# Six weight products in a row on TensorE: five of every six go ahead of all other matmuls in its order

## The chip, the cores and the metric

The kernel runs on one core of one Trainium2 chip. The metric is the device time of one execution in microseconds; the median of several runs counts. Nothing is shared with another core, and there are no collectives.

## The reference

One inference step of a four-layer decoder for two groups of tokens that share the weights: a prompt of 256 tokens and 8 samples of 4 tokens, together 288 columns. Each layer is

```python
x = x + 0.5 * _swiglu(_rmsnorm(x, g0), w_in0, w_out0)
x = x + mixer(_rmsnorm(x, gm))
x = x + 0.5 * _swiglu(_rmsnorm(x, g1), w_in1, w_out1)
```

and the mixer is, by layer, windowed attention with sinks ("swa", layers 0 and 3), the gated delta rule ("gdn", layer 1) and the HGRN2 recurrence ("hgrn", layer 2). The width is 1024, the hidden width of the FFN 2816, everything in 32-bit floats. Every mixer has an input projection, work on heads, states and caches, and an output projection.

## The kernel before

All projections go through one class, `Stream`. A projection is cut into jobs. A job is a column of up to four 128x128 weight tiles ("k tiles") that are multiplied with 288 columns of activations and added up in one PSUM bank. To keep the precision, a weight tile is split into a high part `hi` (ScalarE, line 71) and a rest `lo` (VectorE, line 72), and the activations into `xh` and `xl` likewise; a k tile then takes three products, hi·xh (line 97), hi·xl (line 98) and lo·xh (line 99). So a job of four k tiles is twelve products, and the whole kernel has 16,152 of them. They are called **weight products** here. Up to two jobs ahead are split, three banks (`acc`) take sums, and a finished sum is read by an evacuation function (`evac`) on VectorE, ScalarE or GpSimd.

All other matmuls are called **mixer matmuls**: scores, transposes, decays, states, the inverses of the delta rule, norms. Many of them do not use the whole array. Lines 530, 1190 and 1192 have 64 rows, lines 545, 572, 875, 1167 and 1181 have 64 columns, lines 1098, 1415, 1474 and 1478 have 32. They are called **narrow** here, and those with 128 rows and 128 columns **full**. In the profile a form such as 128*64 is rows * columns of the weights.

The order of each engine's instructions is fixed when the program is built. A list scheduler walks a modelled execution: whenever an engine is free it takes, of the instructions whose inputs are there by the model, the one with the lowest priority number. The number is the place in the program, less an offset where the code sits in `tc.high_priority(offset)`. On the chip each engine then executes its list strictly in that order, and waits where an input is not there yet. `tc.issue_after(ins)` puts instructions behind `ins` in the list of its engine.

The weight products of before stand at their place in the program, without an offset. The mixer work of gdn and hgrn is written after projections that do not depend on it, and raised with offsets: `PRIO = 5000` for the cores of the delta rule and for the heads of hgrn, 6000 to 6500 (`SP`, `QP`, `QG`) for others. So a mixer matmul goes into PE's list as soon as its input is there, between any two weight products. Evacuations, splits and loads have priorities of their own.

Dependencies that matter below: in swa the second half of the output projection (eight jobs) needs all heads; in gdn the last input group (`z1`, 16 jobs) and the first half of the output projection (16 jobs) are left to run beside the cores of heads 4 to 7, and the second half needs those; in hgrn the first half of the output projection (eight jobs) needs heads 0 to 3 and the second half heads 4 to 7. The matmuls of a norm are put behind the products `mms[11]`, `mms[13]` and `mms[25]` of the first eight jobs, where `mms` has the third product of each k tile.

Of the kernel before, what the change touches and what calls it, by code (L numbers as in the profile page):

```python
# [24 lines left out]
class Stream:  # L25
# [3 lines left out]
    def __init__(self, tc, raw, split, psum):  # L29
        self.tc, self.nc, self.raw, self.split_pool, self.psum = tc, tc.nc, raw, split, psum  # L30
        self.chunks, self.jobs = [], []
        self.loaded, self.tiles, self.left = 0, {}, {}
        self.nsplit, self.parts = 0, {}
        self.njob = 0
        self.accs = {}
        self.pooled = set()
        self.held, self.mms, self.tags = [], [], {}
        self.loads = {}
        self.first = 0

    def chunk(self, loads):
        self.chunks.append(loads)
        return len(self.chunks) - 1
# [41 lines left out]
    def run(self, count, hold=False):  # L85
        self.mms = []
        for j in range(self.njob, self.njob + count):
            self.split_to(j + 1 + AHEAD)
            chunk, view, nk, xs, acc, start, stop, evac, m = self.jobs[j]
            hi, lo = self.parts.pop(j)  # L90
            if start:
                self.accs[acc] = self.psum.tile([128, 512], F32, tag=self.tags.pop(acc, "acc"), name="acc")
            ps = self.accs[acc][:m, :T]
            mm = self.nc.tensor.matmul
            last = len(xs) - 1
            for i, (xh, xl) in enumerate(xs):
                mm(ps, hi[:, i, :m], xh(), start=start and i == 0, stop=False)  # L97
                mm(ps, hi[:, i, :m], xl(), start=False, stop=False)  # L98
                self.mms.append(mm(ps, lo[:, i, :m], xh(), start=False, stop=stop and i == last).ins)  # L99
            self.njob += 1  # L100
            if stop and hold:
                self.held.append((evac, self.accs.pop(acc)))
            elif stop:
                evac(self.accs.pop(acc))


PRIO = 5000
# [4 lines left out]
def trunk(ctx: ExitStack, tc: tile.TileContext, I, consts, O):  # L112
# [1547 lines left out]
    for k, run in zip(seq, runs):  # L1660
        if k[0] == "f":
            run()
        else:
            with tc.tile_pool(name="mix", bufs=1, reuse_waits="tile") as M[0]:
                run()
# [92 lines left out]
```

## Time and profile before

| | us |
|---|---|
| median of 3 runs | 2638.93 |
| lowest and highest of them | 2638.28, 2644.87 |
| the profiled execution | 2632.71 |
| its span, first to last instruction | 2630.9 |

PE has 20,268 matmuls, and of these 5384 stand at each of the lines 97, 98 and 99. Times in the rows below are microseconds from the start of the span. PE is the matmuls, PEld the loads of their weights. A matmul's duration in the trace runs over that of the next one, so what one costs is read from the distance between two starts. [...]

### The profile page before, as it was taken

The numbers are of one execution on the slowest core, as the hardware profiler recorded it, in microseconds if no ns is written. First come the engines' busy times: TensorE is split into PE (matmuls) and PEld (weight loads), VectorE is DVE, ScalarE is ACT, GpSimd is POOL, SyncE is SP. The second block draws the span as 40 slices with busy tenths as digits, with TensorE's granted clock in tenths as the row PEclk, the third lists the DMA queues.
The fourth block names the chain that finished last, engine by engine and source line by source line (L and its number), as shares of the span: only waits on it lengthen the run. The fifth ranks groups of instructions, "written<-read, shape, count | busy, mean of one in ns | idle before, by whom it ended". The sixth has DMA issues, their size and how long they took to land.

```text
span 2630.9 us, 52770 instructions
## 1 busy us (share of the span) xinstructions
PE 2549.8 (97%) x20268; PEld 2411.8 (92%) x20268; DVE 1763.5 (67%) x3772; ACT 1414.1 (54%) x3129; POOL 246.4 (9%) x404
## 2 busy tenths in 40 slices
PE   8999999999998899999999999888999999999998
PEld 8999799999997776789999999677999999979998
DVE  6666776576567867667666666877765766667655
ACT  5555655455455456755555545665554555465543
POOL 1000000000002135410000000443000000010000
PEclk9999999999999999999999999999999999999999
DMA  6655245555553354455555555333555565534553
GB/s 188 196 168 172 65 143 164 165 168 161 166 163 97 109 152 136 136 176 159 167 163 163 168 163 160 106 119 122 164 165 164 164 202 177 168 94 121 161 168 124
DMA packets 442609, 400.15 MB, mean 152 GB/s; under 512 B 24730, under 2 KB 440212, under 8 KB 442356
## 3 DMA queue, kind: packets, MB, share of 16 engines
q1 hardware_dynamic: 441732, 395.66, 49.9%
q8 instruction: 159, 2.61, 0.4%
q10 hardware_dynamic: 624, 1.11, 0.1%
q14 instruction: 94, 0.77, 0.1%
HBM read 374.64 MB, written 22.07 MB: 151 GB/s over the span
## 4 chain that ended last, share of the span: by engine, by line
PE 78%; issue 11%; DVE 6%; POOL 2%; ACT 2%; DMA 1%; DVEq 0%; POOLq 0%; ACTq 0%; SPq 0%
PE acc L97 23%; PE acc L99 23%; PE acc L98 23%; DVE lo L72 1%; PE s L545 1%; PE c L530 1%; PE c L1186 0%; DVE W L1400 0%; PE ma L537 0%; PE c L1190 0%; DVE F L1366 0%; PE c L1192 0%; PE c L1181 0%; PE c L1474 0%; ACT hi L71 0%
## 5 line engine op out<-in xcount | busy, mean ns | idle before, releaser
L97 PE MATMUL acc<-sl,hi 128*128 128x288 f32 x5384 | 1612.4, 300 | 13.0 <-ACT sl L1506 2.8
L98 PE MATMUL acc<-sl,hi 128*128 128x288 f32 x5384 | 1606.1, 298 | 1.8 <-DVE sl L1507 1.8
L99 PE MATMUL acc<-sl,lo 128*128 128x288 f32 x5384 | 1600.8, 298 | 2.4 <-DVE lo L72 2.4
L71 ACT ACTIVATE hi<-raw 128x512 fp32r<-128x512 f32 (+1 forms) x1378 | 854.3, 621 | 963.0 <-PE acc L98 934.4
L72 DVE TENSOR_TENSOR lo<-raw,hi 128x512 fp32r<-128x512 f32 (+1 forms) x1378 | 948.4, 689 | 571.2 <-ACT hi L71 515.1
L97 PEld LDWEIGHTS acc<-sl,hi 128*128 128x128 f32 x5384 | 1016.4, 189 | 26.2 <-issue 11.5
L99 PEld LDWEIGHTS acc<-sl,lo 128*128 128x128 f32 x5384 | 1021.2, 190 | 14.6 <-issue 10.0
L98 PEld LDWEIGHTS acc<-sl,hi 128*128 128x128 f32 x5384 | 1018.9, 189 | 12.8 <-issue 9.2
L276 POOL TENSOR_TENSOR r<-v,roots 128x3 f32<-128x3 f32 x5 | 5.8, 1164 | 1847.2 <-DVE v L296 1847.2
L366 DVE TENSOR_TENSOR sil<-acc,sil 128x288 f32<-128x288 f32 x176 | 79.7, 456 | 54.8 <-PE acc L99 51.3
L359 DVE TENSOR_TENSOR sil<-acc,rbc 128x288 f32<-128x288 f32 x176 | 79.6, 456 | 50.1 <-PE acc L99 49.8
L368 DVE TENSOR_TENSOR sl<-sil,sl 128x288 fp32r<-128x288 f32 x176 | 78.9, 452 | 0.0
L360 ACT ACTIVATE sil<-sil 128x288 f32<-128x288 f32 x176 | 77.6, 445 | 2.1 <-DVE sil L359 2.0
L367 ACT ACTIVATE sl<-sil 128x288 fp32r<-128x288 f32 x176 | 77.6, 445 | 0.0
L700 DVE SCALAR_TENSOR_TENSOR acc<-buf,cw,acc 128x312 f32<-128x312 f32 x96 | 59.0, 625 | 11.9 <-ACT acc L698 11.5
L246 ACT ACTIVATE sl<-x,gT 128x288 fp32r<-128x288 f32 x96 | 51.0, 536 | 26.2 <-DVE x L383 15.3
L249 DVE SCALAR_TENSOR_TENSOR sl<-x,gT,sl 128x288 fp32r<-128x288 f32 x96 | 50.5, 530 | 0.1
L262 ACT ACTIVATE sq<-x 128x288 f32<-128x288 f32 x91 | 38.7, 430 | 5.1 <-DVE x L383 5.1
L515 ACT ACTIVATE e<-e,m 128x128 f32<-128x128 f32 (+1 forms) x72 | 32.6, 454 | 16.1 <-DVE m L512 15.8
L1131 POOL TENSOR_TENSOR st<-st,ex 128x512 f32<-128x512 f32 x32 | 37.4, 1190 | 18.1 <-PE ma L1098 18.1
L259 DVE TENSOR_TENSOR ssq<-ssq,sq 128x288 f32<-128x288 f32 x84 | 37.8, 450 | 0.1
L512 DVE CUSTOM_DVE_ANT_0 e<-c,sl,sink 128x128 f32<-128x128 f32 (+1 forms) x72 | 27.8, 418 | 10.6 <-PE c L530 7.7
(435 smaller groups left out, 1823.3 us busy)
## 6 DMA issues: line engine op xcount, KB each, us to landing
raw<-in_ffn_w_in_dram SPq DMA_DIRECT2D x352, 512.0 KB
raw<-in_ffn_w_out_dram SPq DMA_DIRECT2D x128, 512.0 KB
raw<-in_ffn_w_out_dram SPq DMA_DIRECT2D x64, 384.0 KB
raw<-in_gdn_w_in_dram SPq DMA_DIRECT2D x48, 512.0 KB
raw<-in_hgrn_w_in_dram SPq DMA_DIRECT2D x32, 512.0 KB
out_dram<-st SPq DMA_DIRECT2D x24, 512.0 KB
raw<-in_swa_w_in_dram SPq DMA_DIRECT2D x32, 256.0 KB
raw<-in_swa_w_out_dram SPq DMA_DIRECT2D x32, 256.0 KB
```

What stands on the lines that cost most here:

```text
L71: self.nc.scalar.activation(out=h, in_=src, func=AF.Copy)
L72: (self.nc.gpsimd if j in self.pooled else self.nc.vector).tensor_tensor(out=l, in0=src, in1=h, op=ALU.subtract)
L97: mm(ps, hi[:, i, :m], xh(), start=start and i == 0, stop=False)
L98: mm(ps, hi[:, i, :m], xl(), start=False, stop=False)
L99: self.mms.append(mm(ps, lo[:, i, :m], xh(), start=False, stop=stop and i == last).ins)
L246: S.activation(out=h[m], in_=x[:, m], func=AF.Identity, scale=g)
L359: V.tensor_tensor(out=t, in0=ps[:, :T], in1=nrm[key]["rbc"], op=ALU.mult)
L360: S.activation(out=t, in_=t, func=AF.Silu)
L366: V.tensor_tensor(out=t, in0=ps[:, :T], in1=t, op=ALU.mult)
L367: S.activation(out=h, in_=t, func=AF.Copy)
L368: V.tensor_tensor(out=l, in0=t, in1=h, op=ALU.subtract)
L700: V.scalar_tensor_tensor(out=a[:, 0:312], in0=b[:, t:t + 312], scalar=cw[:, 32 * t + mt:32 * t + mt + 1], in1=a[:, 0:312], op0=ALU.mult, o ...
```

## The change

One attribute is added, and the three products of a k tile get offsets:

```diff
+        self.follow = 3 * PRIO
...
             for i, (xh, xl) in enumerate(xs):
-                mm(ps, hi[:, i, :m], xh(), start=start and i == 0, stop=False)
-                mm(ps, hi[:, i, :m], xl(), start=False, stop=False)
-                self.mms.append(mm(ps, lo[:, i, :m], xh(), start=False, stop=stop and i == last).ins)
+
+                with self.tc.high_priority(i % 2 * self.follow):
+                    mm(ps, hi[:, i, :m], xh(), start=start and i == 0, stop=False)
+                with self.tc.high_priority(self.follow):
+                    mm(ps, hi[:, i, :m], xl(), start=False, stop=False)
+                    self.mms.append(mm(ps, lo[:, i, :m], xh(), start=False, stop=stop and i == last).ins)
```

Of the k tiles 0 and 1 of a job, and again of 2 and 3, the first product keeps its place, and the five behind it get an offset of 15,000, more than any mixer work has. Once the first is in PE's list, the other five follow before anything else that is ready. The arithmetic, the number of instructions, the buffers and the DMAs stay as they are. A job of three k tiles is a group of six and one of three.

## Rows read from the trace of the kernel before

**Rows 1.** The page: busy time of each engine, and the chain by engine.
```profile
PE 2549.8 (97%) x20268; PEld 2411.8 (92%) x20268; DVE 1763.5 (67%) x3772; ACT 1414.1 (54%) x3129; POOL 246.4 (9%) x404
PE 78%; issue 11%; DVE 6%; POOL 2%; ACT 2%; DMA 1%; DVEq 0%; POOLq 0%; ACTq 0%; SPq 0%
```

**Rows 2.** Windows: length, busy (instructions) of PE, PEld, DVE, ACT, POOL; PEclk, DMA, GB/s.
```profile
400.00:450.00 50.00, 50.00 (x377) 50.00 (x376) 31.69 (x55) 25.62 (x47) 0.00 (x0) 1.00 0.55 164
...
244.00:341.00 97.00, 93.97 (x715) 76.19 (x714) 64.76 (x231) 54.09 (x165) 10.94 (x20) 0.95 0.32 85
790.00:950.00 160.00, 141.68 (x1499) 121.52 (x1498) 118.15 (x365) 78.96 (x185) 29.08 (x91) 0.95 0.41 111
950.00:1145.00 195.00, 185.99 (x1497) 139.16 (x1496) 138.06 (x332) 134.17 (x460) 94.98 (x148) 1.00 0.51 141
1645.00:1820.00 175.00, 150.43 (x1783) 120.32 (x1782) 138.06 (x345) 112.22 (x355) 70.21 (x96) 0.97 0.39 117
2299.00:2394.00 95.00, 92.18 (x719) 75.08 (x718) 64.30 (x232) 55.28 (x167) 11.80 (x18) 0.96 0.31 84
```

**Rows 3.** Timeline of PE in gdn: start, us, line, tiles, rows*columns, count.
```profile
1064.13 0.30 PE L97 MATMUL acc<-sl,hi 128*128 128x288 f32 x1
...
1064.39 0.38 PE L1116 MATMUL ma<-rh,t 128*128 128x128 f32 x2
1064.53 0.38 PE L99 MATMUL acc<-sl,lo 128*128 128x288 f32 x1
1064.75 0.29 PE L97 MATMUL acc<-sl,hi 128*128 128x288 f32 x1
1064.97 0.66 PE L1181 MATMUL c<-co,sl 128*64 128x128 f32 x8
1065.56 0.40 PE L98 MATMUL acc<-sl,hi 128*128 128x288 f32 x1
1065.80 0.38 PE L1116 MATMUL ma<-rh,t 128*128 128x128 f32 x2
1066.11 0.43 PE L1181 MATMUL c<-co,sl 128*64 128x128 f32 x2
1066.48 0.40 PE L99 MATMUL acc<-sl,lo 128*128 128x288 f32 x1
```

**Rows 4.** Timeline of PEld, the weight loads, in the same stretch.
```profile
1064.13 0.19 PEld L98 LDWEIGHTS acc<-sl,hi 128*128 128x128 f32 x1
...
1065.56 0.19 PEld L98 LDWEIGHTS acc<-sl,hi 128*128 128x128 f32 x1 [0.17 <-issue]
```

**Rows 5.** Timeline of PE: first and last mixer matmuls of the five mixer windows.
```profile
246.94 0.30 PE L485 MATMUL ma<-cst,sl 128*128 128x128 f32 x1 [0.95 <-DVE sl L462]
...
2388.88 0.30 PE L574 MATMUL s<-pt,new 8*64 8x32 f32 x2
```

**Rows 6.** Waits of PE in the whole span: us in total, times, longest us.
```profile
PE c L875 <- DVE sl L880: 8.1, 2, 7.8
PE c L1415 <- DVE W L1400: 5.7, 4, 3.0
...
PE c L1186 <- ACT co L1183: 4.0, 8, 1.3
...
PE ma L1051 <- ACT v L704: 0.2, 1, 0.2
```

**Rows 7.** Timelines: last mixer matmuls of swa, gdn, hgrn (PE), last gating product (POOL).
```profile
334.75 0.42 PE L574 MATMUL s<-pt,new 8*64 8x32 f32 x2
...
1142.27 0.27 PE L1211 MATMUL s<-cst,co 128*128 128x128 f32 x1
...
1150.36 3.19 POOL L1228 TENSOR_TENSOR sl<-sl 128x512 f32<-128x512 f32 x2 [4.65 <-ACT sl L1221]
...
1819.44 0.30 PE L1500 MATMUL s<-lmask,o 128*128 128x32 f32 x2
```

**Rows 8.** Window of 5 us right behind the last matmuls of swa; columns as in Rows 2.
```profile
335.50:340.50 5.00, 5.00 (x22) 5.00 (x22) 1.30 (x3) 0.63 (x1) 0.89 (x2) 0.50 0.05 15
```

## The prediction, made before the change was run

> **What bounds the kernel now.** I read the page first. PE is busy 97% of the span, it carries 78% of the chain that ended last, and no other engine has more than 6% of that chain [rows 1]. So a change of PE's order can move the time, in both directions. Next I read the windows, to see where PE has anything to reorder. In an FFN stretch 377 products take 50 us, 0.133 us each, with PE and PEld busy all the time; nothing else is on PE there, and six in a row are what already runs [rows 2]. The norms' few matmuls are tied to `mms[11]`, `mms[13]` and `mms[25]`, each the last product of a group of six (the fourth, second and second k tile of its job), so their places stay too. What is left are the five mixer windows of together 722 us [rows 2].
>
> Then I followed PE's timeline through these windows, from the first mixer matmul to the last of [rows 5], and counted. The row of weight products is broken 322 times: 46, 40, 112, 75 and 49 times in the five windows in their order. In 209 of these breaks a narrow matmul stands. Only 53 breaks stand at a multiple of six. Of the 321 rows of products between breaks, 209 have fewer than six, on average some 2.5.
>
> **What a break costs.** The excerpt [rows 3] shows both kinds. A full matmul costs its own time and no more: from 1064.39 to 1064.75 two of line 1116 and one product take 0.36 us, which is 0.133 and twice 0.11. Its weights load while the product ahead runs, as a product's do: the load for line 98 starts at 1064.13 with the product of line 97 [rows 3, 4]. A narrow burst costs more at both edges. The product ahead of it takes 0.22 us (1064.75 to 1064.97), 0.09 more than 0.133; the product behind it takes 0.24 us (1065.56 to 1065.80), 0.11 more. Its weights aren't loaded ahead either: PEld idles 0.17 us and starts at 1065.56 together with its own product [rows 4]. Inside, eight narrow ones take 0.59 us and two take 0.37 us (1066.11 to 1066.48), so 0.037 each and 0.30 per burst. If two bursts come to stand at one place, 0.20 us is saved surely, and 0.50 at most, where the two also share the 0.30. I take 0.30, near the lower end, since most neighbours are of different lines and wait for each other's results.
>
> [...]
>
> **The change, part by part.** It adds no instruction, no DMA and no semaphore, and leaves the queues of SP, ACT, DVE and POOL their priorities. It moves products two to six of a group past whatever mixer matmuls were ready, whether these have an offset or not. A mixer matmul that stood within a group now stands up to five products later, by turns 0 to 0.67 us, on average 0.33. Three terms follow.
>
> *Merged breaks, a gain.* If each break moves to the next multiple of six and nothing else moves, the 209 places with narrow matmuls become 153. 56 places times 0.30 us are 17 us (11 to 28 with the ends above). But a delayed matmul delays the one that depends on it, and opens a new break there. That leaves between nothing and all of it; I take half, 8 us.
>
> *Shorter waits, a gain.* PE works its list strictly in order, and the list was made from a model. So PE stands still at mixer matmuls whose inputs come later than modelled: without the one stall at line 875, 55 such waits with together 39 us [rows 6], where the first rows and the last of the list stand. A matmul that is 0.33 us later in the list, behind weight products that are ready, shortens its wait by as much; capped by each row's mean wait this is 18 us. Nothing is gained where the input moves later too. Between 0 and 18 I take 12: line 1415, which weighs most, waits for DVE and POOL work that is late because DVE is busy (138 of 175 us in hgrn [rows 2]), not because PE was late; line 1186 [rows 6] hangs on a chain through PE, and keeps part of its wait. The stall of 7.8 us at line 875 hangs on the solver's long row of steps on DVE; 0.33 us don't touch it. I leave it as it is.
>
> *Work used up early, a loss.* Weight products are what PE does between two links of a mixer chain. If each row of fewer than six, or between two multiples, is filled up, a mixer stage draws products forward: 150, 117, 353, 241 and 164 in the five windows. That costs nothing while independent products are left. Behind the last core of gdn at 1142.27 some 44 products of `z1` are left and 192 of the first half of the output, 236 in all, and the gating that the second half needs ends at 1153.5 [rows 7]. Behind the last head of hgrn at 1819.44 it is 68 and 96, so 164 [rows 7]. Behind the last attention matmul of swa at 334.75 [rows 7] it is only 38, up to the second half of the output projection. In the window from 790 DVE is the busier one in its later part, and the projections that follow are there to fill; nothing is lost. Once the reserve is gone, each further link of the chain leaves PE idle for as long as the mean row filled before. With all rows filled, swa would have done (270+38)/(270+150) = 0.73 of its 46 rows, 12 rows are left, of 270/46 = 5.9 products or 0.78 us each: 10 us, and 10 in the second swa. The same working gives 9 us for the cores of gdn (427 products in 111 rows, 17 rows left) and 7 for hgrn (545 in 75, 7 rows left). That is 36 us, the upper end; zero is the lower. With half of the rows filled, which fits half of the breaks merged, the cores need 176 of 236 and hgrn 120 of 164: nothing. The two swa need 75 and 82 against 38 and lose 4 us each: 8 us.
>
> A wait for a late `lo` stops PE with mixer work queued behind it, but in the strict list of before it did so too: zero, with the waits above as its upper end.
>
> Sum: -8 -12 +8 = **-12 us**. The profiled execution took 2632.7 us, 1.8 more than its span and 6.2 less than the median; so 2620.7 against it, and **2627 us** as a median.
>
> **The rivals.** *The chains are delayed and the reserves run out* (slower). Every row is filled, no break merges, as each link finds its group of six begun. Then 36 us are lost, and of the waits, which sit on the same chains, half is saved, 9 us, where the forecast has 12: +27, 2666 us with everything; with hgrn and gdn keeping their reserve, +20 - 9 = +11, 2650 us. It decides from the point where swa draws more than some 75 products forward in each layer. For it: the short rows are where one link waits for the next. Against it: several heads run side by side, so a delayed matmul finds company.
>
> *The clock* (slower). The granted clock has half-speed stretches in the mixer windows: from the means 0.95, 0.95, 1.00, 0.97 and 0.96 they add up to twice (4.9 + 8 + 0 + 5.3 + 3.8), 44 us [rows 2]. Behind the narrow matmuls that end at 335.1 the clock is 0.50 and a product takes 5.00/22 = 0.227 us [rows 7, 8], so all of them cost up to 44 x (1 - 0.133/0.227) = 18 us. Bigger narrow bursts could bring as many again: -12 + 18 = +6, 2645 us, and more if nothing merges. [...]
>
> *PE isn't what ends these stages* (no change). DVE is busy 138 of 175 us in hgrn and 118 of 160 in the first gdn window [rows 2]. If its chains end the stages, the gains fall into idle time: 2637 us, with what merges in swa and the cores alone eaten by swa's loss. That the order hardly moves, because the model has few mixer matmuls ready together, gives 2639 as well.
>
> *Everything merges* (faster). 17 + 18 us and no loss: 2604 us.
>
> **How the numbers follow.** A measurement of this kernel tells about 0.3%, 8 us, from no change. Forecast (2613 to 2634): 0.50, of which 0.38 below 2631. Everything merges (2600 to 2613): 0.12. PE isn't the end, or the order hardly moves (2632 to 2645): 0.18. Chains delayed (2647 to 2666): 0.14. Clock (2640 to 2655): 0.06, taken as slower. So faster 0.50, within 0.3% 0.30, slower 0.20. The range that leaves out two in ten goes from 2606 to 2652.
>
> **What would show it.** Right: breaks at multiples of six only, some 230 to 280 instead of 322, places with narrow matmuls down from 209 to about 180; the 55 waits well under 39 us; the FFN windows unchanged at 377 products in 50 us; the gain in the windows of gdn's cores and hgrn, little in swa. Wrong: PE idle ahead of the second half of swa's output projection; more than 44 us at half clock; or a new long stall like the one at line 875, since the list is made anew and can set a matmul badly: one of 8 us takes away two thirds of the gain.

## The result, and the profile after

The changed kernel takes **2665.16 us** (median of 4 runs, 2664.38 to 2665.46) where the kernel before took 2640.31 beside it (2638.28 to 2644.87): ratio 1.0091, with a 95% interval from 1.0078 to 1.0104. It is slower, by 25 us. The forecast was 2627, 12 us faster, with a range up to 2652. The forecast was wrong.

The page of the changed kernel, in the order of [rows 1] (busy time and instructions of each engine; the chain by engine; what the granted clock was in 40 slices of 66.6 us each):

```profile
PE 2574.8 (97%) x20268; PEld 2432.2 (91%) x20268; DVE 1751.7 (66%) x3772; ACT 1410.2 (53%) x3129; POOL 237.8 (9%) x404
...
PEclk9999899999999977799999999999999999999999
...
PE 80%; issue 11%; DVE 5%; ACT 2%; POOL 2%; DMA 1%; POOLq 0%; DVEq 0%; ACTq 0%; SPq 0%
```

PE is busy 25.0 us longer than in [rows 1] with as many matmuls, and three slices in the middle have a clock of 0.7. The span is 2663.6 us, 32.7 more than before. The profiled execution of before took 2632.71 us, 7.6 less than the median beside it, that of after 2665.39, its median; that is why 25 us between the medians are 33 between the two traces. A stage that differs by a few us between two traces proves nothing by itself.

Where the time went is read best from the stages, from the first weight product of one to the first of the next. PE's busy time is the union of its matmuls, and half clock the time in which the granted TensorE clock was half of the full one, both added up from the trace's records. The clock records of these two traces (22 before, 32 after) hold 1 and 0.5 of the full clock and nothing between, so a PEclk between in a window is a mean.

| stage | before: us, PE idle, half clock | after: us, PE idle, half clock |
|---|---|---|
| five FFN stretches together | 1699.7, 0.1, 0 | 1699.7, 0.1, 0 |
| swa, first | 123.0, 3.0, 10.2 | 123.5, 2.5, 17.1 |
| gdn | 422.6, 27.9, 17.1 | **466.0**, 39.3, **116.1** |
| hgrn | 238.9, 29.1, 17.1 | **229.5**, 26.5, 10.2 |
| swa, second | 120.5, 2.8, 6.8 | 118.2, 2.1, 6.8 |

The whole loss is in gdn, 43.4 us, and hgrn gains 9.4. The windows of the changed kernel that answer to [rows 2] (length, then busy time and instructions of PE, PEld, DVE, ACT, POOL, then PEclk, DMA share, GB/s; 956 to 1157 and 1157 to 1190 together answer to 950 to 1145, in which the cores of gdn run):

```profile
400.00:450.00 50.00, 50.00 (x377) 50.00 (x377) 31.82 (x56) 25.73 (x48) 0.00 (x0) 1.00 0.54 161
244.00:341.00 97.00, 94.47 (x712) 77.19 (x711) 63.98 (x229) 53.50 (x163) 11.23 (x19) 0.91 0.33 86
790.00:956.00 166.00, 146.03 (x1508) 127.28 (x1508) 118.34 (x365) 79.28 (x183) 28.61 (x93) 0.90 0.42 111
956.00:1157.00 201.00, 182.84 (x1245) 134.52 (x1243) 113.80 (x282) 113.59 (x388) 74.80 (x132) 0.80 0.39 109
1157.00:1190.00 33.00, 32.40 (x258) 25.34 (x255) 24.05 (x55) 23.55 (x75) 11.94 (x12) 1.00 0.54 161
1690.00:1855.00 165.00, 143.21 (x1779) 115.51 (x1779) 138.37 (x343) 110.29 (x350) 69.51 (x94) 0.99 0.41 123
2334.00:2427.00 93.00, 90.90 (x720) 74.80 (x720) 63.54 (x231) 55.36 (x165) 9.76 (x17) 0.96 0.33 88
```

The v projection of gdn (the value heads, 384 products) lies across two of these windows. From its first product to the first product behind it, in the changed kernel and then in the kernel before:

```profile
919.50:1120.50 201.00, 180.39 (x1501) 136.88 (x1499) 106.86 (x263) 105.04 (x337) 68.47 (x140) 0.79 0.44 119
```

```profile
920.90:1083.70 162.80, 153.96 (x1463) 117.83 (x1460) 109.82 (x261) 105.56 (x351) 73.80 (x133) 0.99 0.55 151
```

The v projection is what became slow: 201 us instead of 163, at a clock of 0.79 instead of 0.99, with nearly as many matmuls (1501 and 1463). PE was busy for 180.4 us of it instead of 154.0, 26.4 more, and idle for 20.6 instead of 8.8, 11.8 more.

The order did become what the diff says. The rows of weight products are broken 191 times in the five mixer windows, where the prediction counted 322, and 184 of these breaks stand at a multiple of six; places with narrow matmuls (all forms but 128*128) fell from 209 to 153, the number that the prediction gave for merging in full.

What a slow stretch looks like is plain from PE's timeline (start, us, line, tiles, rows*columns; the products are now at lines 100, 102 and 103, other lines four further on). A product that starts at 1016.13 is the last for 27.7 us:

```profile
1016.13 0.29 PE L103 MATMUL acc<-sl,lo 128*128 128x288 f32 x1
1016.26 0.40 PE L1144 MATMUL ma<-w,km 128*128 128x256 f32 x2
1017.90 0.74 PE L1144 MATMUL ma<-w,km 128*128 128x256 f32 x4 [1.24 <-POOL km L1139]
...
1024.75 1.93 PE L1102 MATMUL ma<-st,sl 128*32 128x256 f32 x16
1026.61 1.01 PE L1185 MATMUL c<-co,sl 128*64 128x128 f32 x8
...
1033.14 1.12 PE L1185 MATMUL c<-co,sl 128*64 128x128 f32 x8
1034.19 0.80 PE L1144 MATMUL ma<-w,km 128*128 128x256 f32 x2
1036.23 0.80 PE L1144 MATMUL ma<-w,km 128*128 128x256 f32 x2 [1.24 <-POOL km L1139]
...
1043.85 0.61 PE L100 MATMUL acc<-sl,hi 128*128 128x288 f32 x1
```

Eight matmuls of line 1185 (line 1181 of before) take 1.05 us here (1033.14 to 1034.19); in [rows 3] eight of them took 0.59. The 16 of line 1102 are recorded with 1.93 us at 1024.75, and elsewhere in the same trace, at 1109.38 and full clock, with 1.07. So PE's chain matmuls run at little more than half speed in this stretch.

Why no product was there is answered by POOL and, in the last row, DVE (same columns):

```profile
1025.91 2.04 POOL L1135 TENSOR_TENSOR st<-st,ex 128x512 f32<-128x512 f32 x2 [1.98 <-PE ma L1102]
...
1028.33 2.04 POOL L1135 TENSOR_TENSOR st<-st,ex 128x512 f32<-128x512 f32 x2
1030.33 1.04 POOL L1139 TENSOR_TENSOR km<-kr,cst 128x512 fp32r<-128x512 f32 x1
1035.14 1.04 POOL L1139 TENSOR_TENSOR km<-kr,cst 128x512 fp32r<-128x512 f32 x1 [3.77 <-PE ma L1144]
1036.14 0.69 POOL L280 TENSOR_TENSOR af<-av,roots 128x2 f32<-128x2 f32 x1
1036.78 0.10 POOL L696 MEMSET buf<- 128x3 f32 x1
...
1040.55 0.41 DVE L698 TENSOR_TENSOR buf<-acc,rbc 128x256 f32<-128x256 f32 x1
```

The products of v's columns 8, 9 and 10 had ended by 1004, 1011 and 1016, and filled the three banks. The evacuation of column 8 needs the buffer that line 696 prepares, and that memset stands on POOL behind the state work of a head (lines 1135, 1139), which hangs on the sample chain on PE (the steps of a head that read and update the samples' state). It came at 1036.78. On DVE the evacuation stood behind the same state work (line 1146) and a core's steps (lines 1199 and 1204), and came at 1040.6; the next product came at 1043.85, in PE's order behind further core matmuls. The two halves of the next weights had been ready since 1011.7. There are four such stretches in v, ahead of columns 3, 7, 11 and 15 (935 to 947, 969 to 980, 1016 to 1044, 1076 to 1106); the longest in the v of before is 5.5 us.

So the heads and the evacuations stand in another order than before, on engines of which the diff says nothing. Why, the runs below found out. In all tables the gdn stage is the one of the profiled execution, and half clock is that of the gdn stage.

### The profile page after: what moved, and what is told of

Same layout as the page of the kernel before. It is cut to its first block, busy times and chain, and to the rows that moved or that the text cites. A ratio compares the mean times of both kernels' runs of the same rounds, so it can differ in the third digit from the quotient of the medians.

```text
span 2663.6 us, 52772 instructions
## 1 busy us (share of the span) xinstructions
PE 2574.8 (97%) x20268; PEld 2432.2 (91%) x20268; DVE 1751.7 (66%) x3772; ACT 1410.2 (53%) x3129; POOL 237.8 (9%) x404
## 4 chain that ended last, share of the span: by engine, by line
PE 80%; issue 11%; DVE 5%; ACT 2%; POOL 2%; DMA 1%; POOLq 0%; DVEq 0%; ACTq 0%; SPq 0%
PE acc L100 24%; PE acc L102 23%; PE acc L103 23%; DVE lo L73 1%; PE c L534 1%; DVE W L1404 1%; PE c L1190 1%; PE c L1194 1%; PE c L1185 1%; PE s L549 1%; PE c L1196 0%; PE ma L541 0%; PE ma L1144 0%; POOL st L1135 0%; DVE F L1370 0%
## 5 line engine op out<-in xcount | busy, mean ns | idle before, releaser
L704 DVE SCALAR_TENSOR_TENSOR acc<-buf,cw,acc 128x312 f32<-128x312 f32 x96 | 52.9, 576 | 12.5 <-ACT acc L702 12.3
L386 DVE TENSOR_TENSOR res<-acc,rh 128x288 f32<-128x288 f32 x64 | 29.0, 453 | 40.7 <-PE acc L103 40.7
```

The costliest lines, as they stand in the source:

```text
L704: V.scalar_tensor_tensor(out=a[:, 0:312], in0=b[:, t:t + 312], scalar=cw[:, 32 * t + mt:32 * t + mt + 1], in1=a[:, 0:312], op0=ALU.mult, o ...
```

## The experiments

### Two runs with offsets in one layer only

The theories at the start were: A, links of the sample chain are delayed by groups of six; B, the clock falls where products are used up early; C, any list that is made anew can be bad. The first two runs set the offset to zero in gdn alone, and everywhere but in gdn.

```diff
         def run():
+            st.follow = 0
...
                 st.run(32 - 2 * KS)
+            st.follow = 3 * PRIO
```

> The change everywhere but in the gdn layer (there all offsets are 0, as before). Common to all theories, from the two traces: the gdn stage alone grew by 43.5 us (777.7 to 1200.3 before, 778.8 to 1244.8 after), hgrn shrank by 9.5, the second swa by 2.2, the first grew by 0.3. If the stages are independent of each other this kernel takes some 11 us less than the one before, about 2629 us. If the loss were spread over the span, or came from code of all stages, it would lie above 2640 us.

Measured: 2656.57 us (2648.55 to 2664.45), ratio 1.0061 [1.0041, 1.0082]; gdn 465.6 us with 112.6 at half clock, hgrn 231.5. **Miss.** In gdn no product had a real offset, and gdn was nearly as slow as with it (the traced execution took 2664.45 us, 8 over the median). Theory A can't be the cause.

The second run had the two values exchanged:

> The change in the gdn layer alone. If the stages are independent: the kernel before plus 43.5 us, about 2684 us, slower than the changed kernel itself. If the gains and losses are not tied to stages: between 2640 and 2665 us.

Measured: 2688.22 us (2678.36 to 2694.09), ratio 1.0177 [1.0152, 1.0202]; gdn 457.0 with 85.3, hgrn 236.8. The number was near the expected one, but not for its reason alone: the FFN stretches between the mixers took 427.3, 426.4 and 426.8 us instead of 424.1, 423.3 and 423.5, with an offset of 0. In PE's list third products there change places with first ones of the next k tile. So `high_priority(0)` around products isn't the same as nothing around them. In gdn PE's list is that of the changed kernel, and still the stage took 457.0 us in this trace and 466.0 in that one: so much can lie between two executions of one order.

### Raising the chain, and a smaller offset

```diff
-        SP = 6000
+        SP = 20000
...
-        CP, VP, RP = 0, 3000, 0
+        CP, VP, RP = 0, 20000, 20000
```

> The changed kernel, but in gdn the units of the sample chain (value transposes, sample unit, state update) get an offset of 20,000, more than the five products' 15,000, so that their matmuls may stand within a group of six. Theory A (links of this chain are delayed by groups of six; eight heads, one after the other, 22 us each before and 28 after): the period goes back to 22 to 24 us and most of the 43.5 us come back, 2622 to 2640 us. Theory B (the half clock in stretches of narrow matmuls is what costs, and the groups bring these stretches about by using up the products early): the cores' matmuls still wait for groups and the three banks still fill early, so at least 60 of the 97 us more at half clock stay, and the time stays above 2650 us. Theory C (the list is made from a model that misjudges, and any new list is as likely bad): no telling, anything from 2630 to 2690 us.

Measured: 2651.42 us (2643.05 to 2654.98), ratio 1.0037 [1.0027, 1.0047]; gdn 453.7 with 88.7. That is far from what theory A expected and just within what theory B did (above 2650 us, at least 60 of the 97 us more at half clock): putting the chain ahead of the products gives back 12 of 43 us.

```diff
-        self.follow = 3 * PRIO
+        self.follow = 1000
```

> The changed kernel with an offset of 1000 in place of 15,000: the five pass only work that has no offset (swa, and in gdn the state update and the convolutions), while raised work (cores of gdn 5000, sample unit 6000, heads of hgrn 5000) may stand within a group as before. Theory A: of the links of the sample chain only those of the state update are still delayed, so the gdn stage loses some 10 to 20 us in place of 43, and the gain in hgrn, whose heads are raised, is gone: 2645 to 2660 us. Theory B: short rows of products between raised matmuls come back, the clock stays up: 2635 to 2645 us. Theory C: anything.

Measured: 2666.58 us (2663.01 to 2667.52), ratio 1.0097 [1.0082, 1.0112]; gdn 457.3 with 75.1, hgrn 237.4. Neither expectation was met. With an offset under that of the heads, hgrn's gain is gone, as theory A has it, but gdn stays slow.

### What an offset of zero changes

The place numbers by which the list is made show what I had overlooked: behind a `high_priority` block the count goes on from where the block began. What stands in a block takes no number, so a number is not simply the place in the program less an offset. In the kernel before the products were nearly all that moved the count on in the v projection, since the evacuations (`conv`, a convolution), heads and sample chains stand in blocks already; in the changed kernel next to nothing does.

```
numbers of the first to the last instruction   before          after
evacuation of v column 0                       7680 to 7692    1824 to 1836
evacuation of v column 1                       7704 to 7716    1824 to 1836
evacuation of v column 2                       7730 to 7742    1826 to 1838
evacuation of v column 3                       7754 to 7770    1826 to 1842
evacuation of v column 5                       7804 to 7816    1828 to 1840
evacuation of v column 7                       7854 to 7870    1830 to 1846
sample chain of head 1, without its offset     7763 to 7795    1835 to 1867
sample chain of head 3, without its offset     7863 to 7895    1839 to 1871
```

Two columns, one head, are 50 numbers apart before and 2 after, while an evacuation is 12 to 16 numbers long and a sample chain 32. So the first steps of a later head get lower numbers than the last steps of an earlier one, on every engine, and heads overtake each other. In PE's list it is seen in how many of gdn's 1560 products stand ahead of the first matmul of each v head:

| kernel | heads 0 to 7 | gdn, half clock |
|---|---|---|
| before | 705, 756, 796, 828, 872, 926, 976, 1022 | 422.6, 17.1 |
| after | 732, 768, **864, 864, 960, 960**, 1012, 1062 | 466.0, 116.1 |
| offset 0 in gdn | 736, 768, **864, 864, 960, 960**, 1012, 1044 | 465.6, 112.6 |
| offset 1000 | 727, 768, **864, 864, 960, 960**, 1012, 1046 | 457.3, 75.1 |
| chain raised | 727, 768, 845, 864, 942, 960, 1005, 1062 | 453.7, 88.7 |

Theory D: the loss comes from the lost count, which brings heads in pairs, and not from the groups. In the next kernels the count is kept by using up numbers behind each k tile:

```diff
+                for _ in range(3):
+                    self.tc.tile_snap_priority()
```

With it, all numbers of other instructions are those of before; with an offset of 0 and this, PE's list is that of the kernel before but for seven places.

### The count lost, and no product moved

This run has the offset 0 everywhere and the count kept everywhere but in gdn.

> The kernel before, with one thing of the change alone, in the gdn layer alone: the products stand in offsets of 0, so that none is moved ahead of anything, but the position counter of the list no longer counts them (12 positions a job in the kernel before, 0 here). Outside the gdn layer the lists are those of the kernel before. A new theory D: the loss comes from the lost count. With it conversions, chains and products of later heads get nearly the same positions as those of earlier heads, so that first steps of a later head overtake last steps of an earlier one; the state heads then come in pairs (v_unit of heads 2 and 3 both behind 864 products, of 4 and 5 both behind 960, where the kernel before has 796, 828, 872 and 926). D expects about the stage that the run with offset 0 in gdn had (465.6 us against 422.6), so 2640 + 43 = 2683 us, 2670 to 2690, with over 80 us of half clock in the gdn stage. Theory A (groups of six delay the chain) and theory B as a consequence of the groups expect the kernel before, 2636 to 2645 us, since no product is grouped here.

Measured: 2668.11 us (2664.96 to 2676.97), ratio 1.0109 [1.0083, 1.0134]; gdn 461.7 with 95.6 at half clock. The median is 2 us under the range; the traced execution took 2676.97, and in it the stage is 39 us longer than in the trace of before. The kernel before, with nothing but the count taken away in one layer, is as slow as the changed one.

### The groups, and no count lost

> The change as the diff words it, with the count kept: five of six products 15000 positions ahead, and behind each k tile three positions are used up, so that every other instruction has the number that it had before. Theory D expects the gdn stage between 415 and 432 us (before 422.6, after 466.0), hgrn at 229 to 232 us and swa as in the changed kernel (118 to 123.5), in sum 2615 to 2640 us, under the kernel before. Theories A and B expect the gdn stage still at 445 us or more and the whole at 2650 us or more, since the grouping and the early use of products are all there. Its list has gdn's products used up earlier than before (the last of the core's state products behind 1260 of 1560 products, 1128 before), so that half clock at the end of the cores, behind 1150 us, would be the early use of products that the prediction priced at 8 us.

Measured: **2624.74 us** (2623.62 to 2629.36) against 2641.57 beside it, ratio 0.9943 [0.9923, 0.9963]; gdn 427.7 with 44.4, hgrn 231.1, swa 119.4 and 118.3. What the diff was meant to do is faster than the kernel before, and only the lost count made it slower. Its windows, an FFN stretch and then the mixer stages up to hgrn (columns as above; those from 955 and 1150 answer to 950 to 1145 in [rows 2]):

```profile
400.00:450.00 50.00, 50.00 (x377) 50.00 (x376) 31.51 (x56) 25.84 (x48) 0.00 (x0) 1.00 0.54 164
244.00:341.00 97.00, 95.20 (x742) 78.32 (x741) 67.87 (x237) 56.49 (x169) 11.76 (x20) 0.95 0.34 93
790.00:955.00 165.00, 144.88 (x1483) 125.43 (x1484) 114.76 (x360) 77.82 (x184) 28.79 (x90) 0.89 0.41 110
955.00:1150.00 195.00, 185.99 (x1503) 142.65 (x1501) 146.31 (x337) 134.49 (x457) 92.35 (x145) 0.98 0.51 143
1150.00:1175.00 25.00, 25.00 (x192) 22.78 (x191) 15.08 (x31) 13.30 (x30) 4.55 (x4) 1.00 0.60 187
1645.00:1820.00 175.00, 153.83 (x1840) 126.43 (x1840) 144.66 (x357) 116.17 (x365) 73.17 (x98) 0.97 0.41 124
```

The 195 us from 955 have PE busy as long as the 195 from 950 in [rows 2], at 0.98. In hgrn's 175 us 1840 matmuls run where [rows 2] has 1783: more work in the same time.

### The groups outside gdn only

The same with the count kept, and offset 0 in gdn.

> The same with the count kept, and in the gdn layer offset 0 as well, so that the gdn list is that of the kernel before to within ten neighbours, while FFN, swa and hgrn stages have five of six products ahead. Theory D expects gdn at 421 to 425 us, hgrn at 229 to 232 us, swa between 118 and 123, in sum 2625 to 2632 us. Against the counted kernel it shows what the grouping itself does in gdn with nothing else changed: if counted is the faster, the prediction's terms for gdn stand; if it is the slower, work used up early or delayed chains cost there.

Measured: 2625.27 us (2621.21 to 2627.34), ratio 0.9938 [0.9918, 0.9958]; gdn 423.0 with 20.5, hgrn 231.8, swa 119.3 and 119.8. As expected. Beside the run before it, the groups in gdn are worth nothing either way by the medians (2624.74 and 2625.27; in the two traces gdn is 4.7 us longer with them); the gain is hgrn's and swa's.

### The cores ahead of the groups

```diff
         def cores(a, b):
-            with tc.high_priority(PRIO):
+            with tc.high_priority(4 * PRIO):
```

> The change with the count kept, and the core units of gdn at 20000 instead of 5000 positions, so that they stand ahead of the grouped products. Its list has the last core's state products behind 1167 of 1560 products at the latest (1260 with the count kept alone, 1128 before), so that more weight products are left beside and behind the cores. If the half clock of 44 us in gdn of the counted kernel is from products used up early, the stage falls from 427.7 to 415 to 424 us, the half clock under 25 us, and the whole to 2612 to 2622 us. If the early use costs nothing there, it stays within 3 us of the counted kernel, 2624.7 us, or above it where the breaks in the groups come back.

Measured: 2624.59 us (2621.49 to 2626.51), ratio 0.9932 [0.9916, 0.9949]; gdn 427.4 with 47.8. The second case came: the time stayed, and so did the half clock. In the counted kernel it doesn't lie at the end of the cores (1.00 from 1150 in its windows): 27.3 of the 44.4 us lie ahead of v, where the list of before had 13.7 us in its own trace and 27.3 in another (the run after the next, which has that list up to v but for one batch of seven matmuls). Using the products up early costs nothing that can be seen.

### A third of the count

> The run with the lost count in gdn alone, with a third of the count given back: one position for each k tile, 4 a job instead of 0 or 12. No product is moved ahead. Its list has the v heads evenly spread again (v_unit of heads 1 to 5 behind 739, 794, 842, 892 and 936 products). Theory D (later heads overtake earlier ones only where positions do not advance) expects the gdn stage at 418 to 432 us and the whole at 2633 to 2650 us. If what costs is any difference from the positions before (a list that happens to be bad), it stays near the run without count, 461.7 us and 2668 us.

Measured: 2663.01 us (2659.67 to 2667.14), ratio 1.0082 [1.0066, 1.0099]; gdn 452.2 with 64.9. **Half a miss.** The v part took 163.6 us, as before (162.8), so the even heads brought v back. But the 16 jobs ahead of it took 69.8 instead of 45.1 us. PE's waits between 880 and 960 show where (us in total, times, longest):

```profile
PE c L881 <- DVE sl L886: 17.1, 2, 15.8
```

This is the stall at line 875 of [rows 6], 8.1 us before: with other numbers PE's list puts that matmul still earlier, behind 480 of gdn's products instead of 576, and it waits the longer for the DVE steps that it hangs on. So pairs of heads are one way in which numbers cost time, and not the only one.

### The count lost in v only

The kernel before, with the count stopped for the 32 jobs of v.

> The kernel before, with the count lost only for the 32 jobs of v in the gdn layer (4 us of products in 33 or so), no product moved ahead, everything else with the numbers that it had. Up to v the list is that of the kernel before; in v the heads come in pairs (864, 864 and 960, 960). Theory D expects the part up to v as before (143 us from the first gates to the first product of v), the v part near 199 us against 162.8, the gdn stage at 455 to 465 us, the whole at 2670 to 2685 us. If the loss without count comes from other places than the pairs (as in the run with a third of the count, where a stall ahead of v took it), the stage stays under 435 us.

Measured: 2671.57 us (2670.97 to 2674.43), ratio 1.0128 [1.0112, 1.0145]; gdn 462.7 with 99.0. v took 190.2 us against 162.8, less than expected, and the group behind it 73.1 against 64.5. Four of its windows of 20 us in v:

```profile
995.00:1015.00 20.00, 18.04 (x145) 14.61 (x143) 14.77 (x31) 11.70 (x36) 4.72 (x6) 0.98 0.39 112
1015.00:1035.00 20.00, 17.69 (x90) 10.62 (x89) 7.32 (x19) 9.24 (x35) 7.67 (x13) 0.50 0.40 106
...
1055.00:1075.00 20.00, 17.51 (x143) 13.86 (x143) 14.77 (x32) 12.18 (x36) 6.13 (x9) 1.00 0.40 112
1075.00:1095.00 20.00, 17.69 (x91) 10.64 (x89) 7.20 (x20) 9.38 (x35) 7.67 (x13) 0.51 0.40 106
```

The rhythm of pairs: 20 us at full clock with some 144 matmuls, 20 us at half clock with 90. Up to v it took 148 us instead of 143 with the same list (but for one batch of seven matmuls) and twice the half clock, 27.3 us against 13.7. Most of the loss, 36 of 40 us, is in v and the group behind it, and the pairs are in v.

### What the clock has of it

Is the half clock the cause of the loss, or does it only go with the pairs? To find out, full products that nobody reads are put into the banks of the v heads and sample chains, where in the changed kernel they leave the pairs as they are (864, 864 and 960, 960). Each stands in a bank that the real matmul behind it starts anew.

```diff
+        def fill(ps, n):
+            xh = xs_of(key, range(1))[0][0]()
+            for _ in range(n):
+                PE.matmul(ps[:, 0:T], xh[:, 0:128], xh)
...
             ps = misc()
+            fill(ps, FILL)
             for b in range(8):
                 a = b % 4
                 PE.matmul(ps[32 * a:32 * a + 32, 0:256], kqm[:, 32 * b:32 * b + 32],
```

> The changed kernel with 256 added 128 x 288 products that nobody reads, four ahead of the first work in each of the 64 PSUM banks that the v heads and sample chains of gdn take. At 0.133 us each they are 34 us of PE at full clock. The list keeps the heads in pairs (864, 864 and 960, 960). If half clock is the cause of the loss of 43 us in gdn and not only its companion, they raise the granted clock in the stretches without products (116 us of half clock in the stage before this), and the stage comes out at or under 466 us, near 440 to 460, although 34 us of work are added. If the loss is the order of the heads alone, with the clock following, the stage gets longer by a good part of the 34 us, to 480 to 500 us, whatever the clock does.

Measured in the changed kernel: 2662.11 us (2659.44 to 2667.76), ratio 1.0081 [1.0064, 1.0098]; gdn 465.3 with 41.0 at half clock, 75 less than without the added products, at the same length. That is at the border between the two expectations, so the price of the added products had to be known. The same products in the kernel before:

> The kernel before with the same 256 added products that nobody reads, four ahead of the first work in each of the 64 banks of v heads and sample chains, 34 us of PE at full clock. Its heads stay evenly spread (742, 757, 815, 849, 909), and there was little half clock to be won back in gdn (17.1 us). It gives the price of the added products. If they cost 20 to 34 us here (gdn at 442 to 457 us), then the 75 us of half clock that they removed in the changed kernel, whose stage stayed the same, gave as much back, and the lower clock was part of the loss. If they are hidden in idle PE time (gdn at 421 to 430 us), the removed half clock gave back next to nothing, and the pairs of heads are the whole loss.

Measured: 2679.12 us (2676.56 to 2681.95), ratio 1.0156 [1.0135, 1.0177]; gdn 464.9 with 47.8, 42.3 us longer than without them. The v parts of the two, the changed kernel first:

```profile
917.50:1113.50 196.00, 181.64 (x1674) 143.20 (x1673) 114.40 (x272) 107.97 (x351) 71.24 (x143) 0.96 0.44 122
```

```profile
925.20:1143.30 218.10, 207.77 (x1882) 162.12 (x1880) 127.31 (x308) 126.08 (x411) 79.52 (x147) 0.95 0.44 120
```

In the kernel before the added products cost all that they are and a little more; the half clock rose there, and the heads, still spread, moved a little (heads 2 and 3 behind 757 and 815 products instead of 796 and 828). In the changed kernel they bring 173 matmuls more into 5 us less (1674 in 196, 1501 in 201), with the clock at 0.96 instead of 0.79. Over the whole stage, 34 us of added work lengthened PE's busy time by 6.4 us (from 426.8 to 433.2), and its idle time fell from 39.3 to 32.1. So the half clock was a good part of the loss: some 28 of the 43 us, an estimate from 34 less 6.4, which is near the 32 us by which PE is busy longer in gdn than before. The rest, 11 us, is idle time of PE (39.3 against 27.9). That division rests on single traces; a kernel with pairs, full clock and no added work wasn't to be had.

## Why the prediction was wrong

**The step that failed** is one sentence: that the change "leaves the queues of SP, ACT, DVE and POOL their priorities". It costed the edit as if only the products had new numbers. The block in which they now stand takes away the 12 numbers of every job, and with them the distance by which all other instructions were ordered. With the count kept, the same edit gives 2624.74 us, 16.8 less than the kernel before beside it; with the count lost and no product moved, 2668.11, 26.5 more.

**Merged breaks (8 us).** All merged, not half: 191 breaks and 153 narrow places after. With the count kept it is 218 and 172, so 37 places times the prediction's 0.30 us, 11 us. Hgrn shows a gain in PE's busy time: 205.7 us with the count kept against 209.8, and the whole stage at 229.5 to 231.8 us in the seven runs with groups there, against 237.8 to 241.3 in the five whose hgrn list is that of before.

**Shorter waits (12 us).** This term was three times too large. The waits of mixer matmuls apart from the stall at line 875 add up to 39.3 us (55 waits) before and 35.2 (52) with the count kept, 4 us less in one trace of each. After, all together, they are 52.1 (65), with these on top:

```profile
PE c L1419 <- DVE W L1404: 9.1, 7, 2.9
...
PE ma L1144 <- POOL km L1139: 6.2, 6, 1.2
...
PE c L1190 <- ACT co L1187: 4.4, 4, 3.1
```

Line 1415 of [rows 6], now 1419, did not get shorter waits. That fits inputs that moved with the matmuls, as the prediction feared for the capped sum and then took too little account of; no run separates it from other reasons.

**Work used up early (8 us).** It cost nothing where I had put it: the two swa stages got some 3 us shorter each (118.2 to 121.1 with groups but for one at 123.5, 120.5 to 126.0 with the list of before). The 236 products behind gdn's cores were no cover for v: the stream of products is strictly in order, and with three banks full none of the later ones started, however many were left (27.7 us from 1016.13 in the changed kernel). The reserve beside the chain was what the three banks in front could take, not what the program still held. That is the second thing that the prediction did not see.

**The sum** of the three (-12) came near what the edit gives with the count kept (-16.8), but by luck, since its parts were off in both directions: -11, -4 and 0 for -8, -12 and +8. By stage hgrn has some -8, each swa -3, gdn nothing.

**The rivals.** The clock was given 6% and 18 us, at 0.41 us for each us of half clock (18 of 44; the records of before hold 51.2 us of 0.5 in the four mixer stages). The price was good: in v, PE is busy 26.4 us longer with 83 us more of half clock (86.4 against 3.4), which is 0.32. The amount was not: gdn alone went from 17.1 to 116.1 us. And it came another way than thought, not with bigger bursts but with stretches without any product (0.55 from 1080 to 1100). Adding dense products brought the clock in v from 0.79 to 0.96. Half clock didn't come with an idle PE: where the count was lost in v only, a window at 0.50 had PE busy for 17.69 of its 20 us, with narrow matmuls. "Chains delayed and reserves run out" has the nearest time, 2650 to 2666, and not the cause: no link is delayed by a group where no product is grouped, and that run is as slow. "PE isn't what ends these stages" doesn't hold for hgrn, which got 7 to 9 us shorter although DVE is busy 144.66 of 175 us there. "Everything merges" came true of the breaks, and not of the time. That the list is made anew and "can set a matmul badly" stood among what would make the prediction wrong, and this is its kind, on a larger scale.

**What showed it.** Of the signs named, FFN windows unchanged and gain in hgrn came true; the gain in gdn's cores and the shorter waits did not; "more than 44 us at half clock" (155 us in the whole trace, 58 in that of before) was the sign that it went wrong.

## What to carry to other kernels

Where a list is ordered by place numbers and offsets, an edit that puts instructions into an offset block changes the numbers of everything behind it. Before costing such an edit by what it moves, ask what else is numbered by it, and compare the order of the other engines and of the chains: heads in pairs are seen there without a run. With the count kept, the groups of six bring this kernel to 2624.7 us. And of work kept to run beside a chain, count only what can start: in this ordered stream with three banks, that was three sums.

## What was not expected of the hardware

Half clock came with PE busy. Two windows of the changed kernel (columns as above), the first with weight products between the narrow matmuls, the second without any:

```profile
1000.00:1020.00 20.00, 18.10 (x149) 14.58 (x148) 14.74 (x32) 12.27 (x39) 4.64 (x6) 1.00 0.41 112
...
1080.00:1100.00 20.00, 16.82 (x86) 10.14 (x85) 7.23 (x19) 10.28 (x37) 8.75 (x13) 0.55 0.40 106
```

PE is busy 18.10 and 16.82 of 20 us, and the granted clock is 1.00 and 0.55. The chain of narrow matmuls takes the longer for it in such a stretch (1.05 us for eight of line 1185 against 0.59 in [rows 3]). That a stretch without weight products so prolongs itself is my estimate from these two numbers; no run shows it alone. The stretch from 1016 stands here ahead of the one that answers to it with the added products:

```profile
1016.00:1044.00 28.00, 22.96 (x129) 14.69 (x127) 11.82 (x30) 13.28 (x48) 10.10 (x18) 0.64 0.45 123
```

```profile
1015.00:1043.00 28.00, 25.35 (x207) 18.22 (x206) 15.50 (x41) 16.59 (x58) 13.48 (x29) 1.00 0.47 126
```

With 78 matmuls more it is no longer, at the full clock. All in all the 256 products that compute nothing, 34 us of work, were free in the changed kernel (gdn 465.3 us with them, 466.0 without), while in the kernel before, with 17 us of half clock in gdn to begin with, they cost 42 us.
